# The second gate of an adaLN layer: from TensorE to VectorE's products in the down projection, with four engine orders laid out anew

## The chip, the cores and the metric

The kernel runs on one core of one Trainium2 chip. The metric is the device time of one execution in microseconds (us), the median of the runs shown.

## The reference

One layer of a diffusion backbone on 128 context tokens and 512 latent tokens of width 1024, all in fp32. A conditioning vector for each kind of token (c for the latent ones, c_ctx for the context) gives six modulation vectors of 1024; the last of them, g2, scales the output of the feed-forward part:

```python
mod = jax.nn.silu(cond) @ prm["w_ada"] + prm["b_ada"]
sh1, sc1, g1, sh2, sc2, g2 = [m[:, None, :] for m in jnp.split(mod, 6, axis=-1)]
h = rms_norm(x, prm["norm_mix_pre"]) * (1 + sc1) + sh1
...   # input projection, SSD mixer and Conformer branch -> mix = [y_ssd, u] @ w_out
x = x + g1 * rms_norm(mix, prm["norm_mix_post"])
h = rms_norm(x, prm["norm_ffn_pre"]) * (1 + sc2) + sh2
up = dwconv(h @ prm["w_ffn_up"])          # 2 x 2816 channels, 3x3 taps (latent), width 3 (context)
f_gate, f_val = jnp.split(up, 2, axis=-1)
f = (jax.nn.silu(f_gate) * f_val) @ prm["w_ffn_down"]
x = x + g2 * rms_norm(f, prm["norm_ffn_post"])
```

So g2 is needed only where the down projection's sums are scaled, at the very end. `w_ada` is 1024 x 6144.

## The kernel before

Channels lie on the 128 partitions, tokens on the free axis: T = 640 columns, 512 latent and 128 context. A fp32 product is three TensorE products of a high and a low part. Each weight unit (128x1024 or 128x768) is loaded by SP into a buffer `wr` (two of them), copied by ScalarE to `wh` (the high part, line 311) and subtracted by GpSimd (POOL) to `wl` (the low part, line 313); both have three buffers. Units are numbered in the order of use: 48 to 64 belong to the output projection, 65 to 108 to the up projection, 109 to 132 to the down projection.

The stages in the trace: input projection, SSD and convolutions until about 380 us; output projection until 492; the second normalisation (class `Mid`), with the first five up units woven in, until 542; up projection until 807, each unit followed by a convolution of nine taps (`up_conv`: the first tap by ScalarE, line 1227, the others by DVE, lines 1237 to 1240) which reads the unit's PSUM tile, of which there are three; down projection until 960; then the last normalisation, residual and the stores.

The modulation is computed in halves of 512 columns. `ada_load(i, tags)` loads eight tiles of 128x512 (256 KB each) of `wada2`; `ada_half(i, ws)` makes 64 small products on TensorE (line 460) with the activated conditioning (`cts`), copies the sum (line 463, `adar`), transposes it on TensorE (line 423) and adds the bias on DVE (line 432) into `modv[:, 48, 2]`. Halves 0 to 5 run in the output projection. Halves 6 and 7 are g2: half 6 is loaded into S0 to S7 and computed in the second normalisation, half 7 is loaded into H8 to H15 during the up projection and computed at its unit 11. `gg2` is g2 times the gain `g_ffn_post`, made by one DVE instruction. In `down_out(m)` ScalarE takes the Square of a finished tile (line 1412) and copies it scaled by `gg2[:, m, c]` (line 1418), for eight tiles m = 0 to 7 of 128 output channels.

The order of the instructions of each engine is not that of the program. `ORDER` holds a list for PE, DVE, Activation, Pool and SP, with the numbers of the program's instructions in the order in which the engine is to issue them, and `issue_in_order` chains them in this order. So an instruction that has to wait holds everything behind it on its engine.

Of the kernel before, what the change touches and what calls it, by code (L numbers as in the profile page):

```python
# [37 lines left out]
for _name, _w in (("b_ada", 48), ("g_mix_pre", 8), ("g_mix_post", 8), ("g_ffn_pre", 8),  # L38
# [48 lines left out]
3440-3442 3449-3451 3493-3504 3509-3510 3444-3445 3452 3511-3513 3539-3556 3455-3470 3477-3492 3514-3524  # L87
3505-3508 3557-3570 3525-3538 3453-3454 3572-3575 3644-3647 3668-3669 3576-3578 3648-3650 3670-3674
3579-3581 3571 3651-3653 3582-3584 3654-3656 3675-3680 3585-3587 3657-3659 3681-3682 3620-3623 3588-3590
3624-3625 3591-3593 3596-3598 3594-3595 3599-3619 3626-3643 3660-3667 3683-4059 4061-4081 4060 4082-5548  # L90
5597-5615 5549-5596 5616-5658 5693-5695 5659-5664 5696-5716 5665-5692 5717-6599 6665-6668 6600-6664
6669-6676""",
# [10 lines left out]
448-450 405-407 443 408-410 421-422 444 411 424 423 451 445-446 412-413 426 414-415 425 427 454 429-430 455  # L103
452-453 434 439 436 438 435 456 433 457 437 440 460 431 459 458 461-462 441 466-467 469-470 472 478 473
475-476 468 479-480 482-485 481 471 474 488 477 486 489 487 495 498 496 502 501 497 491 490 505 508 494
499-500 515 509 503-504 518 492 512 493 519 506-507 510-511 520-522 537 523 513-514 516 525 527-528 530 526
529 532-533 538 531 535 524 540 534 557 536 539 517 541-543 545 544 558 546 548 550 547 559 552 560-561
563-564 566 549 551 567 565 553 568 554-556 569 571-575 570 562 576-585 589 586-588 593 590 594 591-592 595
597 596 598 601-602 599-600 605 603-604 606-612 615-616 613-614 617-749 1053 750-1046 1049-1051 1047-1048
1052 1054-1063 1065 1064 1066-1075""",  # L110
# [15 lines left out]
477 442 440 416-417 478 427 419 413 428 420 418 421-424 479 425 480 443 426 482 481 483 465 449 451 450  # L126
452-453 455 454 484-485 457 469-470 487 459 486 456 466 460 468 458 461-462 467 463-464 488-489 492 490 495
498-499 494 502 496 491 497 493 505-506 509 500-501 503 507 510-511 504 512-514 516 515 508 525-526 528-529
527 521 517-518 532 519-520 531 523 522 524 530 542 541 533-536 544 543 550 537 545 538-540 547 546 559 551
548 553-554 560 556 555 549 552 557-558 561-565 568-569 566-567 570 578 571-577 581 579 583 580 603-605  # L130
609-611 582 584 588 585 615-616 632 617 586 621-622 633 590 589 634 587 643-644 638 592 623 591 645 639-640
596 593 649 624 650 598 594 597 601 599 651 595 652 606 600 602 613 607 612 608 618 614 625 619-620 627 626
630 628-629 635 631 641 636-637 646 642 653 647-648 655 654 658 656-657 660 659 663 661-662 665 664 668
666-667 670 669 673 671 675 672 674 678 676 680 677 679 683 681 685 682 684 688 686 690 687 689 693 691 695
692 694 698 696 700 697 699 703 701 727 705 702 704 708 706 709 707 714 710-713 715 719 716 725-726 717 720
731 718 723 721-722 732 724 728-729 733-734 730 735 741 736-740 745 742-744 746-747 751 748-750 752-753 757
754-756 758-759 763 760-762 764-765 769 766-768 770-771 775 772-774 776-784""",
# [1459 lines left out]
```

## Time and profile before

| what | us |
| --- | --- |
| median of 3 runs (lowest, highest) | 984.08 (983.13, 984.47) |
| span of the profiled execution | 979.4 |
| busy: PE, DVE, ACT, POOL | 944.5, 686.9, 471.3, 577.9 |
| share of PE in the chain that ended last | 87% |

The span is the time from the first to the last instruction of the profiled execution; what an execution takes outside it is in the runs' times alone, 4.7 us here by the difference to the median. Times of rows count from the span's start. PE is TensorE, DVE VectorE, ACT ScalarE, POOL GpSimd, SP the engine that issues the transfers. A name like `wh<-wr` says that a tile of the group `wh` is written from one of `wr`; numbers are left out.

### The profile page before, as it was taken

The numbers are of one execution on the slowest core, as the hardware profiler recorded it, in microseconds if no ns is written. First come the engines' busy times: TensorE is split into PE (matmuls) and PEld (weight loads), VectorE is DVE, ScalarE is ACT, GpSimd is POOL, SyncE is SP. The second block draws the span as 40 slices with busy tenths as digits, with TensorE's granted clock in tenths as the row PEclk, the third lists the DMA queues.
The fourth block names the chain that finished last, engine by engine and source line by source line (L and its number), as shares of the span: only waits on it lengthen the run. The fifth ranks groups of instructions, "written<-read, shape, count | busy, mean of one in ns | idle before, by whom it ended". The sixth has DMA issues, their size and how long they took to land.

```text
span 979.4 us, 18795 instructions
## 1 busy us (share of the span) xinstructions
PE 944.5 (96%) x7623; PEld 920.9 (94%) x7623; DVE 686.9 (70%) x1076; ACT 471.3 (48%) x799; POOL 577.9 (59%) x416
## 2 busy tenths in 40 slices
PE   4999999999999999999999999999999999999995
PEld 3799999999999998998889999999999999999995
DVE  1769898999989997523585998998988898400004
ACT  4355666877668477622464852323232336322211
POOL 1334699889999882534662994444454436543434
PEclk9999999999999999999999999999999999999998
DMA  9622424433424422578662322222222231322213
GB/s 347 250 72 86 117 82 127 146 95 123 139 80 142 128 91 93 196 244 303 200 218 88 129 86 69 84 78 73 86 66 86 66 87 54 94 69 76 82 38 108
DMA packets 50294, 117.52 MB, mean 120 GB/s; under 512 B 6016, under 2 KB 13952, under 8 KB 50208
## 3 DMA queue, kind: packets, MB, share of 16 engines
q1 hardware_dynamic: 50208, 116.33, 37.2%
q8 instruction: 60, 0.98, 0.4%
q14 instruction: 26, 0.21, 0.1%
HBM read 112.55 MB, written 3.75 MB: 119 GB/s over the span
## 4 chain that ended last, share of the span: by engine, by line
PE 87%; DMA 3%; ACT 3%; DVE 2%; SPq 1%; POOL 1%; issue 1%; POOLq 0%; ACTq 0%; DVEq 0%
PE ps L415 72%; PE ps L1259 3%; PE pq L415 2%; PE pq L818 2%; PE pq L807 1%; PE pq L460 1%; SPq L452 1%; DMA wr<-in_wout 1%; PE pq L744 1%; PE pq L441 1%; POOL wl L313 1%; PE pq L473 1%; DMA S<-acD 1%; ACT wh L311 1%; DMA T<-in_wada 1%
## 5 line engine op out<-in xcount | busy, mean ns | idle before, releaser
L313 POOL TENSOR_TENSOR wl<-wr,wh 128x1024 fp32r<-128x1024 f32 (+3 forms) x127 | 290.4, 2290 | 316.3 <-ACT wh L311 299.2
L415 PE MATMUL ps<-H,wh 128*128 128x384 f32 (+1 forms) x1636 | 315.7, 309 | 0.1
L311 ACT ACTIVATE wh<-wr 128x1024 fp32r<-128x1024 f32 (+3 forms) x131 | 131.3, 1003 | 316.2 <-PE ps L415 183.2
L415 PE MATMUL ps<-T,wh 128*128 128x384 f32 (+1 forms) x1472 | 272.5, 306 | 1.8 <-ACT S L1227 1.8
L1237 DVE SCALAR_TENSOR_TENSOR S<-ps,prms,S 128x441 f32<-128x441 f32 (+2 forms) x336 | 233.5, 695 | 29.4 <-ACT S L1227 18.9
L415 PEld LDWEIGHTS ps<-H,wh 128*128 128x128 f32 x1636 | 249.0, 188 | 2.7 <-issue 1.7
L415 PEld LDWEIGHTS ps<-T,wh 128*128 128x128 f32 x1472 | 218.9, 188 | 2.2 <-ACT S L1227 2.1
L872 DVE SCALAR_TENSOR_TENSOR ps<-u,prms,ps 128x655 f32<-128x655 f32 x205 | 185.1, 903 | 10.8 <-ACT ps L869 4.8
L415 PE MATMUL ps<-H,wl 128*128 128x384 f32 (+1 forms) x818 | 191.8, 309 | 0.0
L415 PE MATMUL ps<-T,wl 128*128 128x384 f32 (+1 forms) x736 | 166.2, 305 | 0.0
L415 PEld LDWEIGHTS ps<-H,wl 128*128 128x128 f32 x818 | 129.0, 188 | 1.0 <-issue 1.0
L415 PEld LDWEIGHTS ps<-T,wl 128*128 128x128 f32 x736 | 113.0, 188 | 0.0
L488 DVE RECIPROCAL rsm<-rsm 128x160 f32<-128x160 f32 (+2 forms) x9 | 7.4, 817 | 147.1 <-ACT rsm L487 147.1
L415 PE MATMUL ps<-S,wh 128*128 128x384 f32 (+1 forms) x420 | 88.0, 310 | 1.6 <-ACT wh L311 1.6
L415 PEld LDWEIGHTS ps<-S,wh 128*128 128x128 f32 x420 | 66.5, 188 | 2.8 <-ACT wh L311 1.8
L415 PE MATMUL ps<-S,wl 128*128 128x384 f32 (+1 forms) x210 | 54.9, 309 | 0.3 <-POOL wl L313 0.3
L789 ACT ACTIVATE S<-S,AC 128x128 f32<-128x128 f32 x140 | 45.5, 392 | 2.4 <-DMA S<-acD 2.4
L885 POOL TENSOR_TENSOR T<-T,T 128x640 f32<-128x640 f32 x20 | 32.0, 1602 | 12.5 <-ACT T L881 12.5
L1227 ACT ACTIVATE S<-ps,prms 128x640 f32<-128x640 f32 x42 | 36.5, 869 | 0.0
L415 PEld LDWEIGHTS ps<-S,wl 128*128 128x128 f32 x210 | 35.2, 188 | 0.9 <-POOL wl L313 0.5
L881 ACT ACTIVATE T<-u,prms 128x512 f32<-128x512 f32 (+1 forms) x54 | 27.9, 554 | 6.8 <-POOL T L885 6.8
L1339 POOL TENSOR_TENSOR H<-S,S 128x640 f32<-128x640 f32 x16 | 25.3, 1581 | 0.0
(346 smaller groups left out, 1180.3 us busy)
## 6 DMA issues: line engine op xcount, KB each, us to landing
wr<-in_wup SPq DMA_DIRECT2D x44, 512.0 KB, 3.5
wr<-in_win SPq DMA_DIRECT2D x36, 512.0 KB, 3.9
T<-in_wada SPq DMA_DIRECT2D x49, 256.0 KB, 5.4
S<-acD SPq DMA_DIRECT2D x28, 320.0 KB, 4.7
wr<-in_wdown SPq DMA_DIRECT2D x16, 512.0 KB, 3.4
wr<-in_wout SPq DMA_DIRECT2D x13, 512.0 KB, 4.5
H<-in_wada SPq DMA_DIRECT2D x23, 256.0 KB, 4.6
S<-in_wada SPq DMA_DIRECT2D x16, 256.0 KB, 5.4
```

Source lines behind the costliest of these rows:

```text
L311: ac.activation(hi[:, :n], raw[:, :n], AF.Copy)
L313: lo_eng.tensor_tensor(lo[:, :n], raw[:, :n], hi[:, :n].bitcast(F32), SUB)
L415: last_mm[0] = te.matmul(out, w, x[:, c0:c1], start=first and i == 0, stop=last and i == 2)
L789: ac.activation(rc, rc, AF.Relu, scale=-1.0, bias=AC2[:, c, row:row + 1])
L818: te.matmul(py[64 * h:64 * h + 64, i * P:(i + 1) * P], xt[:, c * P + 64 * h:c * P + 64 * h + 64], rs[h, d][:, c * P:(c + 1) * P], start=d ...
L872: ve.scalar_tensor_tensor(acc, u[:, j:j + UO], w(j), acc, MUL, ADD)
L881: ac.activation(t[:, b:c], u[:, a:a + c - b], AF.Copy, scale=w(j))
L885: gp.tensor_tensor(far, far, t, ADD)
L1227: ac.activation(out, v, AF.Identity, bias=prm_col("ffn_b", i), scale=w(1, 1))
L1237: ve.scalar_tensor_tensor(ob, vl[:, r0 + a - 1:r1 + a - 1, q0 + b - 1:q1 + b - 1], w(a, b), ob, MUL, ADD)
L1259: te.matmul(pt[:, o:o + c1 - c0], w[k] if i in (1, 2) else w[:, k * P:(k + 1) * P], x[:, c0:c1], start=k == 0 and j == 0, stop=k == KD - 1 ...
L1339: gp.tensor_tensor(f_raw[q], a, b, MUL)
```

## The change

Halves 6 and 7 of the modulation leave TensorE. In their place DVE computes g2 in the down projection: for each m, the 128 columns of `w_ada` that belong to its channels come transposed (channels on the partitions, 1024 conditioning inputs on the free axis, two loads of 128x512), and for each of the two conditioning vectors two instructions multiply them by the activated vector, broadcast to all partitions, and sum along the row (`accum_out`). So there are 32 such products, 8 sums of the two halves with the bias, and 8 scalings by the gain.

```diff
-    ada_w2 = ada_load(6, [f"S{k}" for k in range(8)])
...
-    ada_half(6, ada_w2)
...
+    def cond_rows():
+        for c in range(2):
+            for h in range(2):
+                t = slot(("S16", "S17", "U0", "U1")[2 * c + h])[:, 0:512]
+                src = idhl_d[P + 32 * c + 16 * h:P + 32 * c + 16 * h + 16, :].rearrange("a b -> (a b)")
+                sy.dma_start(t, src.unsqueeze(0).to_broadcast([P, 512]))
+                ac.activation(t, t, AF.Silu)
+                crows.append(t)
...
-        if i == 11:
-            g2_rest = ada_half(7, ada_w2, now=False)
-        if i == 14:
-            g2_rest()
-        if i == 5:
-            ada_w2 = ada_load(7, [f"H{8 + k}" for k in range(8)])
+        if i == 32:
+            cond_rows()
...
-    ve.tensor_tensor(gg2, modv[:, 40:48, :], prm_col("g_ffn_post", 0, 8).unsqueeze(2).to_broadcast([P, 8, 2]), MUL)
+    junk = sm.tile([P, T], F32, tag="tanh", name="junk", bufs=1)
+    gate_ws = []
+
+    def gate_load(m):
+        ws = []
+        for h in range(2):
+            t = slot((("S8", "S9") if m else ("H5", "H6"))[h])
+            sy.dma_start(t[:, 0:512], wada2[6 + m // 4, 2 * (m % 4) + h])
+            ws.append(t)
+        gate_ws.append(ws)
+
+    def gate_rows(m):
+        for c in range(2):
+            for h, w in enumerate(gate_ws[m]):
+                ve.scalar_tensor_tensor(junk[:, 0:512], w[:, 0:512], 1.0, crows[2 * c + h], MUL, MUL,
+                                        accum_out=modv[:, 2 * m + h, c:c + 1])
+        ve.scalar_tensor_tensor(modv[:, 40 + m, :], modv[:, 2 * m, :], prm_col("b_ada", 40 + m), modv[:, 2 * m + 1, :],
+                                ADD, ADD)
+        ve.tensor_scalar(gg2[:, m, :], modv[:, 40 + m, :], prm_col("g_ffn_post", m), None, MUL)
+        if 0 < m < KD - 1:
+            gate_load(m + 1)
+
...
+                i = DOWN_ORDER.index((m, g))
+                if i == 1:
+                    gate_load(0)
+                    gate_load(1)
+                for j in {3: (0,), 4: (1,), 5: (2, 3), 6: (4, 5), 7: (6, 7)}.get(i, ()):
+                    gate_rows(j)
```

On the host, c and c_ctx are appended to the input `idhl`, and the last two halves of `wada2` are transposed.

The lists in `ORDER` change from the output projection on. PE's list only loses the 66 instructions of halves 6 and 7. What the other lists do at the places that matter here, counted by instruction:

- ACT, output projection: the two copies `AT<-pq` (line 1030) that stood behind an activation of `T` into S13 (line 985) stand ahead of it. Second normalisation: the first tap of the first up convolution (S10, line 1227) stands ahead of the copy of weight unit 70, not behind it. Down projection: the scaled copies move behind later weight copies, that for m=1 ahead of `wh120`, that for m=2 ahead of `wh122`, and the Square of m=3 ahead of `wh122` too.
- DVE: the products of the gate stand behind one another, m=1 to m=7 without other work between; the scaling for m=1 comes within the products of m=5, the scaling for m=2 behind the last product of m=7. Those of m=0 lie between the taps of the last convolution. The tail's multiplications come first and its additions later.
- SP, output projection: the store of `nsb` (from S13) stands four places earlier; three of the `T` loads of `wada2` go earlier, six other loads go behind the load of weight unit 51. Down projection: the loads of the gate's halves stand between those of weight units 107 and 122; those of m=7 directly ahead of unit 122's.
- POOL: the additions to `m2sq` stand behind later weight units; the rest is nearly as before.

## Rows read from the trace of the kernel before

**Rows 1.** The page, parts 1 and 4: busy us; shares of the chain.

```profile
PE 944.5 (96%) x7623; PEld 920.9 (94%) x7623; DVE 686.9 (70%) x1076; ACT 471.3 (48%) x799; POOL 577.9 (59%) x416
...
PE 87%; DMA 3%; ACT 3%; DVE 2%; SPq 1%; POOL 1%; issue 1%; POOLq 0%; ACTq 0%; DVEq 0%
```

**Rows 2.** Windows by stage: length, busy us by engine, clock, DMA share.

```profile
420.00:492.00 72.00, 67.97 (x717) 64.11 (x715) 29.47 (x50) 26.32 (x44) 36.31 (x24) 1.00 0.73 244
...
591.00:640.00 49.00, 49.00 (x392) 48.60 (x392) 43.81 (x73) 15.86 (x19) 21.52 (x10) 1.00 0.23 76
...
850.00:905.00 55.00, 55.00 (x385) 55.00 (x384) 0.00 (x0) 13.18 (x18) 22.86 (x13) 1.00 0.28 80
```

**Rows 3.** Chain that ended last, 500 to 600: start, us, what.

```profile
517.31 1.08 PE pq L460 x33
...
522.39 1.00 PE pq L460 x28
...
529.22 0.11 PE pq L423
...
591.28 1.89 PE pq L460 x64
593.17 3.25 PE ps L415 x21
```

**Rows 4.** Timeline of PE; in brackets the idle time before.

```profile
399.97 1.30 PE L460 MATMUL pq<-H,cts 128*32 128x128 f32 x40 [0.98 <-ACT AT L1030]
...
454.70 0.97 PE L460 MATMUL pq<-T,cts 128*32 128x128 f32 x24 [0.74 <-DMA T<-in_wada]
...
457.34 0.52 PE L460 MATMUL pq<-T,cts 128*32 128x128 f32 x10 [1.03 <-DMA T<-in_wada]
...
533.66 0.28 PE L1259 MATMUL ps<-T,wh 128*128 128x256 f32 x1
...
542.49 0.82 PE L415 MATMUL ps<-T,wh 128*128 128x384 f32 x4 [1.76 <-ACT S L1227]
```

**Rows 5.** Timeline of ScalarE.

```profile
398.67 0.92 ACT L985 ACTIVATE S<-T,prms 128x640 fp32r<-128x640 f32 x1 [1.78 <-DMA out_nsb<-S]
...
534.03 1.06 ACT L311 ACTIVATE wh<-wr 128x1024 fp32r<-128x1024 f32 x1 [3.60 <-issue]
535.00 0.87 ACT L1227 ACTIVATE S<-ps,prms 128x640 f32<-128x640 f32 x1
```

**Rows 6.** Timeline of DVE.

```profile
531.06 0.60 DVE L1183 SCALAR_TENSOR_TENSOR T<-U,modv,T 128x128 fp32r<-128x128 f32 x2
...
535.90 5.81 DVE L1237 SCALAR_TENSOR_TENSOR S<-ps,prms,S 128x441 f32<-128x441 f32 x8 [4.23 <-ACT S L1227]
...
542.00 0.35 DVE L1240 SCALAR_TENSOR_TENSOR S<-ps,prms,S 128x127 f32<-128x127 f32 x1
...
586.67 0.35 DVE L1240 SCALAR_TENSOR_TENSOR S<-ps,prms,S 128x127 f32<-128x127 f32 x1
...
821.32 7.49 DVE L402 TENSOR_TENSOR H<-H,H 128x640 fp32r<-128x640 f32 x4
...
841.98 0.83 DVE L402 TENSOR_TENSOR H<-S,H 128x640 fp32r<-128x640 f32 x1
```

**Rows 7.** DMA issues: KB each, median us to landing; quiet stretch, then down projection.

```profile
S<-in_wada SPq DMA_DIRECT2D x2, 256.0 KB, 2.7
...
wr<-in_wdown SPq DMA_DIRECT2D x14, 512.0 KB, 3.4
```

**Rows 8.** Groups of DVE by shape: busy us, mean ns of one.

```profile
L574 DVE SCALAR_TENSOR_TENSOR S<-tanh,S 128x640 f32<-128x640 f32 x6 | 4.9, 824 | 1.3 <-ACT tanh L573 1.3
```

**Rows 9.** Timelines of ScalarE and POOL in the down projection.

```profile
890.50 0.69 ACT L1412 ACTIVATE AT<-ps 128x640 f32<-128x640 f32 x1
...
896.64 1.06 ACT L311 ACTIVATE wh<-wr 128x1024 fp32r<-128x1024 f32 x1 [4.62 <-issue]
...
885.71 2.41 POOL L313 TENSOR_TENSOR wl<-wr,wh 128x1024 fp32r<-128x1024 f32 x1 [4.48 <-ACT wh L311]
```

More of the change, by code (lines that the diff above doesn't have):

```diff
@@ L107 @@
[L107 to L110, printed above, removed]
+448-450 405-407 443 451 408-410 421-422 445 411 424 444 446 423 412 427 413 426 414-415 425 454 429 455 430
+452-453 438 433-434 456 437 435 457 436 439 458 460 459 440 461 431 462 441 466 478 467 469-470 472-473 475
@@ new lines @@
+468 476 479-480 483 482 484-485 474 481 471 477 487 486 490 488-489 495 498 496-497 491 501 494 505 502 492
+508 499-500 509 503-504 506 518 512 493 507 515 519 510-511 520-522 537 523 513 525 527 514 528 530 516 532
+529 526 517 533 531 538 535 524 536 534 540 557 539 541-543 545 544 558 546 548 550 547 559 549 551-553
+560-561 555 554 563-564 566-569 565 556 571-572 562 574 573 570 575-587 590 589 594 588 593 591-592 595-596
+599 597 601-602 598 600 603 606 604 607 610 605 608 614 613 609 612 611 615-633 635 634 636-653 655 654
@@ new lines @@
+656-659 665 660-661 666 662-664 667-673 675-676 674 677-683 685-687 684 688-693 695 694 696-702 705 703-704
+706-752 755 753 756 754 757-772 775 773-774 776-793 795-796 794 797-810 815 811-813 816 814 817-822 825 823
+826 824 827-833 835 834 836-842 845 843 846 844 847-851 855 852-854 856-863 865-866 864 867-881 885 882-884
+886-890 895 891-892 896 893 897-898 894 899-900 905 901 906 902-904 907-913 915-916 914 917-930 935 931-932
+936-937 933 938 934 939-943 945-949 944 950-952 955-959 953-954 960-973 975 974 976-981 1045 982-990 1049
@@ new lines @@
+991 995 992-994 996-1001 1005 1002-1003 1006-1010 1004 1011-1014 1019-1022 1015 1017 1016 1023 1018 1024
+1029 1025-1026 1031 1030 1032-1033 1027 1034 1028 1035 1047 1046 1036-1039 1050 1040-1042 1051-1052 1043
+1053 1044 1048 1054-1059 1061-1064 1067-1070 1073 1071 1074-1075 1072 1076 1065 1077 1079 1078 1080-1081
+1060 1082-1083 1085-1086 1084 1087-1088 1091-1094 1066 1089 1095-1096 1090 1097-1098 1100 1102 1099 1104
+1106 1101 1108 1103 1105 1109 1111 1113 1115 1107 1117 1110 1112 1116 1114 1118""",
@@ L130 @@
[L130 to L134, printed above, removed]
@@ new lines @@
+625 628 618 626 633 629 627 639 634 644 635 640 651 645-646 652-654 656 658 657 659 661 655 660 662-664 666
+668 665 667 671 669-670 673 672 674 676 678 677 679 681 675 687 682 680 688 690 689 691-693 695-697 700 698
+694 701 699 729 703 702 706 705 708 707 710 704 709 711 716 712 727 714 713 721 717-718 715 723 720 719 722
+733 725 728 724 731 734 726 730 735-736 732 738 737 740 743 747 744 748 750 749 739 745 753-754 746 756 751
+755 752 741 759 757-758 760 762-763 761 742 764-768 771 769 772 770 773-774 777-778 780-781 779 775 782
@@ L138 @@
+785-786 783 776 784""",
     "Pool": """
@@ L1548, in _layout @@
     out["cst"] = cst
-    out["idhl"] = np.concatenate([np.eye(32, dtype=f32)] * 4, axis=0)
+    out["idhl"] = np.concatenate([np.eye(32, dtype=f32)] * 4 + [a["c"][0].reshape(32, 32), a["c_ctx"].reshape(32, 32)])
     w = a["w_ada"][0].reshape(4, 2, P, 6, 4, 2, P)
@@ L1554, in _layout @@
     w = a["w_ada"][0].reshape(KD, P, 6, 2, 512)[:, :, 2:6]
-    out["wada2"] = w.transpose(2, 3, 0, 1, 4).reshape(8, KD, P, 512)
+    w2 = w.transpose(2, 3, 0, 1, 4).reshape(8, KD, P, 512)
+    g2 = a["w_ada"][0][:, 5 * D:].T.reshape(KD, P, 2, 512).transpose(0, 2, 1, 3).reshape(2, KD, P, 512)
+    out["wada2"] = np.concatenate([w2[0:6], g2])
     w = a["w_in"][0]
```

57 lines of the change are left out of this document (27 added, 30 removed).

## The prediction

> **What bounds the kernel now.** I read the page first: its busy times and its chain. TensorE is busy for 944.5 us of a span of 979.4, and 87% of the chain that ended last is PE [rows 1]. So a microsecond taken from PE's own stream counts wherever PE never waits. The windows by stage say where that is: from 591 to 640 and from 850 to 905 PE is busy for the whole window (the stretches between are alike), and in the second of these DVE does nothing at all, while DMA moves at a share of 0.28 [rows 2]. In the output projection PE loses 4 of 72 us and DMA stands at 0.73. Third come PE's own waits in order of time. They lie where an activation, a load or the first convolution is late [rows 4]; the last before the down projection's end is at 542.49. Last I followed the two new orders, instruction by instruction, against these times.
>
> **PE work removed, half 7.** Its 64 small products take 1.89 us in the chain at 591.28 [rows 3]; the transposition that goes with them I price like that of half 6, 0.11. PE is full afterwards [rows 2], and DVE keeps pace: PE takes the tile of its next unit at 593.17 [rows 3], and the convolution that frees it (three units back) had ended at 587.0 [rows 6], 6 us before. So nothing else fills the gap: **-2.0 us**.
>
> **Half 6 and the wait at 542.49.** The products lie in two pieces, 1.08 and 1.00, and the transposition takes 0.11 [rows 3]: 2.2. Behind them PE waits 1.76 for its sixth up unit [rows 4], which needs the PSUM tile that the first convolution reads; DVE leaves that tile at 542.00 + 0.35 [rows 6]. The convolution starts at 535.90, behind ScalarE's first tap (535.00, 0.87), which stands behind the copy of a weight unit (534.03, 1.06) [rows 5]. The new ACT order has the tap ahead of the copy, so the convolution starts 0.94 earlier by itself and 2.2 earlier because PE reaches the tile's end earlier: 3.1 at most. DVE's normalisation of the second half runs beside the last piece; its last tile is ready at 531.06 + 0.60 [rows 6] and PE takes it at 533.66 [rows 4], 2.0 later. 1.1 of this goes with the last piece and the transposition, and the new order has DVE make some of the eight tiles up to three instructions later (0.8 us): at most 0.9 is lost. I take **-3.0** (bounds -2.2 and -3.1).
>
> **Output projection.** Here only the orders change. Waits that they touch: 0.98 at 399.97, where PE waits for a copy that ScalarE makes late because it sat 1.78 on a store [rows 4, 5]; the new ACT order has the copies ahead of that activation, and SP issues the store four places earlier. At 454.70 and 457.34 PE waits 0.74 and 1.03 for conditioning weights [rows 4]; the new SP order lets three of these loads go earlier, but it puts six others behind a unit's load, in a stage where DMA is busy three quarters of the time [rows 2]. Sum of what can go: 0.98 + 0.74 + 1.03 = 2.75; everything named and 0.7 of small gaps around it give 5. If the moved loads are late instead, one more wait of the size of 1.03. I take **-2.0** (bounds +1 and -5).
>
> **Second gate on DVE: what is added.** 32 products of 128x512 with a row sum, 8 small sums, 8 scalings; 16 loads of 256 KB, the same in number and size as the removed ones; four broadcast loads and four Silu, issued near 600 us where ACT has 33 us idle in 49 [rows 2] and the needed slots are free: 0. The nearest row to the product is L574, also two SBUF sources into SBUF: 0.824 us for 640 columns [rows 8]; the same operation with 127 columns takes 0.35 [rows 6], so a column costs 0.92 ns and 512 columns 0.71. The row sum is shown by no row; from below it costs nothing, from above it doubles the streamed part (0.47 more). I take 0.71, since the same operation without it is the nearest.
>
> All this lies beside PE if the chain is in time. It is one chain: from m=1 all loads go into the same two slots, so each pair waits for the four products of the pair before. One round: issue 0.4, landing 3.4 (a 512 KB unit's time in this stage [rows 7], the upper bound; 2.7 for two quiet loads of this size is the lower), then three products that don't overlap the landing, 2.1, sums and semaphores 0.35: 6.3. DVE is free at 842.8 [rows 6]. First round with all four products: 842.8 + 3.9 + 2.9 = 849.6; six more give 887.4, and the scaling for m=2, which the new DVE order puts behind the last product of m=7, comes near **889**.
>
> Who waits: in ACT's new order the scaled copy for m=2 stands ahead of the split of weight unit 122, and so does the Square of m=3, which PE's end of that tile allows at 890.50 [rows 9]. Queued behind them: the copy of unit 122 (1.06), then its low part on POOL (2.41), then PE, which starts that unit at 896.64, when the buffer of unit 121 comes free [rows 9]. Backward: 896.6 - 2.4 - 1.1 - 0.65 (the scaled copy) = 892.4 at the latest, so 3.4 us of slack. On SP the load of unit 122 stands behind the loads of m=7 (about 882), lands by 886, and is in time. The other scaled copies have more room (m=1 about 5 us).
>
> What can eat the 3.4: DVE and POOL. At 821.32 four DVE subtractions with both sources in SBUF, beside a busy POOL, take 7.49 us, against 0.83 for one of them at 841.98 [rows 6]; so 4.2 us are lost in 7.5. In the chain DVE works for 45% of a round and POOL for 22 of 46 us (nine units of 2.41 or less [rows 9]); lost share 0.56 x 22 x 0.45 = 5.5 us. Against it the lower landing gives 7 x 0.7 = 4.9. An estimate of both: 0 to 2 us of stall. I take **+0.8** (bounds 0 and +3, without the half rate below).
>
> The Trainium skill, "SBUF — State Buffer", section "Who interferes with whom", calls the port that DVE and GpSimd share an exclusive lock; the trace agrees in kind (7.49 us for four). By it alone the products would lose all of POOL's time that falls into their part of a round, 22 x 0.45 = 9.9, and the stall would be 9.9 - 4.9 - 3.4 = 1.6 instead of 0.8, the time 978.7; by the row's share it is 0 to 2.
>
> **Tail.** Reordered, same work: the adds later, the multiplications first. 0 (bounds -0.5 and +0.5).
>
> **Sum.** -2.0 - 3.0 - 2.0 + 0.8 + 0 = -6.2. The profiled execution's span is 979.4; the median of the runs shown, 984.08, lies 4.7 above it, and I let these 4.7 stand. 984.1 - 6.2 = **977.9 us**. From no change one can tell about 0.2%, 2.0 us.
>
> **Rivals.** (1) *The chain at half rate: slower.* If the product with a row sum runs at half speed, 0.47 more each, some 25 of the 28 products count in full (three a round and the first): 889 + 11.8 = 900.8. DVE then works for 60% of a round and loses 0.56 x 22 x 0.6 = 7.4 to POOL, against 4.9 from the loads: 903.3, 10.9 past 892.4. PE stalls there once by 10.9; with the rest at -7.0 the time is 984.1 + 3.9 = 988. It decides from about 1.0 us a product on, where the stall reaches the 7.0. For it: the row of L574 has no row sum. Against it: the same two sources at full rate, 0.824 for 640 [rows 8].
>
> The Trainium skill has this as a rule: "Vector Engine (DVE) Microarchitecture Reference", section "7. Points that are easy to get wrong", says that this instruction with two sources in SBUF that are not bf16 halves its throughput, as no port is left for the accumulator. L574's 0.824 us speaks against it for instructions without a row sum; none here shows one with it.
>
> (2) *The orders of the output projection give nothing, or cost.* The gain there is 0 and the chain costs 2: -2.0 - 2.6 + 0 + 2 = -2.6, 981.5, still faster. For it: DMA at 0.73, with loads moved behind others. (3) *All given back:* loads moved behind others cost 1 more, and the chain's stall is 3: -4.6 + 1 + 3 = -0.6, 983.5, the same. (4) *More than forecast:* the whole 5 of the projection, no stall: -10, 974. (5) *The removed products cost nothing on PE* (another wait takes their place): against it stands that PE is full from 591 on, so half 7 must show; I leave it inside (3).
>
> **How the numbers follow.** The forecast, 975 to 980, 0.60; (2), 980 to 982, 0.12; (3) 0.09; (4), below 975, 0.07; (1) 0.12. Faster by over 0.2%: 0.60 + 0.12 + 0.07 = 0.79; same 0.09; slower 0.12. The range leaves out the half rate (0.12) and the far end of (4) (0.03): 974 to 985, and the time itself is that of the forecast.
>
> **What would show it.** Right: no L460 rows after 500; PE's wait before its sixth up unit gone or below 1, and the unit some 3 us earlier beside the end of the output projection; the up projection shorter by 2.0 at 591; the new DVE products at 0.7 to 0.85 between 805 and 885, PE without a gap or with one below 2 near unit 122; the first stage boundary after the output projection 1 to 4 us earlier. Wrong: products above 1.1 us; a PE wait for ScalarE's split near 885 to 900 by over 4; loads of conditioning weights later at 450 to 460 than before; a convolution start that does not move.

## The result: slower by 0.5%

The changed kernel takes 986.60 us (median of 7 runs, 984.54 to 991.53), the kernel before 982.62 on the same chip (7 runs, 979.07 to 984.47). The ratio is 1.0046, 95% interval 1.0026 to 1.0066: slower, where 977.9 and faster were predicted, and outside the range of 974 to 985. The profiled execution of the changed kernel spans 983.7 us and took 985.5, so 1.8 lie outside a span and not 4.7 (1.8 to 2.0 in every run here). The profile of before (979.4) must then be an execution of about 981.2, quicker than before's median.

First the page of the changed kernel, parts 1 and 4, against [rows 1].

```profile
PE 943.2 (96%) x7493; PEld 919.2 (93%) x7493; DVE 709.6 (72%) x1151; ACT 472.8 (48%) x801; POOL 576.0 (59%) x416
...
PE 79%; DMA 8%; DVE 5%; ACT 4%; issue 1%; POOL 1%; SPq 1%; DVEq 0%; ACTq 0%; POOLq 0%
```

PE has 130 instructions less and yet only 1.3 us less of busy time: some of those that are left ran longer. And its share of the chain fell from 87% to 79%. So work left PE, and waits and slower stretches came. Where, shows PE's timeline (start, duration, and in brackets the wait ahead of it):

```profile
403.65 0.42 PE L470 MATMUL pq<-H,cts 128*32 128x128 f32 x8 [0.85 <-DMA H<-in_wada]
...
433.93 0.44 PE L425 MATMUL ps<-S,wl 128*128 128x384 f32 x1 [0.44 <-POOL wl L323]
...
446.80 0.86 PE L470 MATMUL pq<-T,cts 128*32 128x128 f32 x24 [0.47 <-DMA T<-in_wada]
...
485.62 0.50 PE L425 MATMUL ps<-S,wh 128*128 128x256 f32 x2 [1.92 <-ACT wh L321]
...
488.58 0.39 PE L425 MATMUL ps<-S,wl 128*128 128x256 f32 x1 [0.68 <-POOL wl L323]
...
492.69 0.39 PE L425 MATMUL ps<-S,wh 128*128 128x256 f32 x1 [2.07 <-DVE M L1168]
...
545.78 0.82 PE L425 MATMUL ps<-T,wh 128*128 128x384 f32 x4 [0.88 <-DVE S L1250]
...
843.32 0.56 PE L425 MATMUL pq<-S,wh 128*128 128x384 f32 x2 [0.56 <-DVE S L412]
```

Against [rows 4]: the wait of 1.76 before the sixth up unit is 0.88 now, as forecast. The waits of 0.98, 0.74 and 1.03 in the output projection are not gone: others stand in their place (0.85, 0.44 and 0.47 are shown; with 0.27 at 441.51 and 0.22 at 458.58 they sum to 2.25 of the 2.75). The waits at 485.62 and 488.58 (1.92 and 0.68) were there before, somewhat shorter:

```profile
483.45 0.50 PE L415 MATMUL ps<-S,wh 128*128 128x256 f32 x2 [1.59 <-ACT wh L311]
...
486.01 0.39 PE L415 MATMUL ps<-S,wl 128*128 128x256 f32 x1 [0.28 <-POOL wl L313]
```

New are 492.69 and 843.32.

A second reading is used throughout below, the *offset*: both programs have the same PE instructions apart from the removed ones, so each one's start can be compared with its start in the profile of before. The sixth up unit, for example, starts at 542.49 before and 545.78 after: +3.29. Each row is one execution, each column a time of before; "end" is the span's end.

| kernel | 380 | 480 | 498 | 542 | 600 | 841 | 905 | end |
| --- | --- | --- | --- | --- | --- | --- | --- | --- |
| after | +3.0 | +1.8 | +6.4 | +3.3 | +0.8 | +0.8 | +2.6 | +4.3 |
| e5, no products | +2.1 | +2.2 | +5.1 | +2.0 | -0.3 | -0.2 | -0.2 | +1.6 |
| e9, gate chain laid out anew | +5.8 | +5.6 | +8.7 | +5.6 | +3.3 | +3.3 | +4.2 | +5.9 |
| e11, before's orders, new program | -0.4 | -0.4 | +0.0 | -1.9 | -4.2 | -4.2 | -4.2 | -3.3 |
| e12, halves 6 and 7 left out of before | -0.4 | -1.6 | -1.0 | -2.9 | -3.6 | -3.6 | -3.6 | -2.8 |
| e13, e11 with new projection orders | +1.1 | +2.7 | +5.7 | +3.7 | +2.8 | +2.8 | +2.8 | +3.3 |

What stands at 345 (+2.7 in after, -0.4 to +2.6 in the others) is chance: no instruction ahead of it was changed. The new orders begin a little ahead of the output projection, on DVE at 351 and on ScalarE and SP by 372; from 345 to 380 most executions with them lose 0.3 to 0.5 (e8 1.6, e9 3.2), those with before's orders there at most 0.1. Only the differences between columns are read. After loses 4.6 between 480 and 498, gains 3.1 until 542 and 2.5 until 600, loses 1.8 between 841 and 905 and 1.7 in the tail.

### The profile page after: what moved, and what is told of

The parts are those of the page before. It is cut to its first block, busy times and chain, and to the rows that moved or that the text cites. A ratio compares the mean times of both kernels' runs of the same rounds, so it can differ in the third digit from the quotient of the medians.

```text
span 983.7 us, 18619 instructions
## 1 busy us (share of the span) xinstructions
PE 943.2 (96%) x7493; PEld 919.2 (93%) x7493; DVE 709.6 (72%) x1151; ACT 472.8 (48%) x801; POOL 576.0 (59%) x416
## 4 chain that ended last, share of the span: by engine, by line
PE 79%; DMA 8%; DVE 5%; ACT 4%; issue 1%; POOL 1%; SPq 1%; DVEq 0%; ACTq 0%; POOLq 0%
PE ps L425 67%; PE ps L1269 3%; DMA H<-in_wada 2%; DMA T<-in_wada 2%; PE pq L828 2%; PE pq L817 1%; DMA wr<-in_wout 1%; PE pq L754 1%; DMA S<-acD 1%; PE pq L425 1%; ACT wh L321 1%; DVE S L1247 1%; POOL wl L323 1%; DMA S<-in_wada 1%; DMA T<-in_xT 1%
## 5 line engine op out<-in xcount | busy, mean ns | idle before, releaser
L1419 DVE SCALAR_TENSOR_TENSOR junk<-S,S 128x512 f32<-128x512 f32 x14 | 13.5, 962 | 25.2 <-DMA S<-in_wada 25.1
```

The source lines that it names most:

```text
L1419: ve.scalar_tensor_tensor(junk[:, 0:512], w[:, 0:512], 1.0, crows[2 * c + h], MUL, MUL, accum_out=modv[:, 2 * m + h, c:c + 1])
```

## The experiments

All times are medians in us, with the lowest, the highest and the number of runs; ratios are to the kernel before on the same chip.

| run | time | ratio, 95% interval |
| --- | --- | --- |
| after | 986.60 (984.54-991.53, 7) | 1.0046 [1.0026, 1.0066] |
| e1_copy_first | 992.24 (986.22-996.88, 6) | 1.0085 [1.0057, 1.0113] |
| e2_tail_before | 988.51 (983.82-993.10, 9) | 1.0055 [1.0033, 1.0077] |
| e3_gate0_later | 987.59 (981.65-991.50, 11) | 1.0043 [1.0023, 1.0063] |
| e4_all_three | 985.64 (979.75-992.75, 12) | 1.0027 [1.0006, 1.0049] |
| e5_no_products | 982.90 (980.35-984.94, 12) | 0.9996 [0.9982, 1.0010] |
| e6_orders_alone | 989.24 (988.09-995.25, 6) | 1.0075 [1.0055, 1.0095] |
| e7_load_ahead | 985.60 (982.05-991.18, 12) | 1.0028 [1.0011, 1.0045] |
| e8_four_edits | 981.48 (978.97-985.05, 12) | 0.9986 [0.9974, 0.9999] |
| e9_deadline | 983.75 (981.44-987.09, 12) | 1.0006 [0.9990, 1.0022] |
| e10_five_edits | 980.84 (978.17-982.23, 12) | 0.9975 [0.9959, 0.9990] |
| e11_old_front | 978.31 (975.82-983.11, 12) | 0.9955 [0.9938, 0.9972] |
| e12_halves_out | 978.51 (975.93-983.17, 12) | 0.9958 [0.9941, 0.9975] |
| e13_new_oproj | 984.22 (981.65-986.32, 12) | 1.0012 [0.9998, 1.0026] |
| e14_new_up | 978.21 (975.80-980.54, 9) | 0.9954 [0.9938, 0.9970] |
| e15_new_tail | 980.25 (977.50-983.35, 12) | 0.9975 [0.9961, 0.9989] |
| e16_new_to480 | 980.97 (977.60-984.71, 12) | 0.9981 [0.9960, 1.0002] |
| e17_new_480 | 981.91 (980.10-984.94, 12) | 0.9997 [0.9978, 1.0016] |
| e18_copy_ahead | 981.38 (979.46-985.61, 12) | 0.9989 [0.9970, 1.0008] |

My theory after the first result: the removed work is worth what was predicted, and the new orders give it back at three places (ScalarE's copy of weight unit 63 at 490, the first gate products between the last convolution's taps at 843, the tail), with a stall of the gate chain besides. The rival: the 32 products on DVE cost it, wherever they stand.

### Three places, one at a time (e1 to e4)

e1 moves ScalarE's copy of weight unit 63 (529) ahead of three squares of the residual (521, 518, 520), where before had it; e2 gives the tail before's order on all four queues; e3 puts the products for m=0 behind the last convolution's work; e4 is the three together.

```diff
 e1, "Activation":
-... 528 521 518 520 529 519
+... 528-529 521 518 520 519
 e2, "DVE", and likewise the ends of "Activation", "Pool" and "SP":
-... 1098 1100 1102 1099 1104 1106 1101 1108 1103 1105 1109 1111 1113 1115 1107 1117 1110 1112 1116 1114 1118
+... 1098-1106 1108 1107 1109-1118
 e3, "DVE":
-... 990 1049 991 ... 1039 1050 1040-1042 1051-1052 1043 1053 1044 1048 1054
+... 990-991 ... 1039-1044 1048-1054
```

> The changed kernel with one instruction moved: ScalarE's copy of weight unit 63 stands again ahead of the three squares of the second normalisation, where the kernel before has it. Theory A (the copy is what PE waits for at 492.69; the squares hold it while DVE's additions are slowed beside POOL, and after the wait PE's clock falls): PE's wait of 2.07 us there shrinks below 0.5, the granted clock between 489 and 498 stays at 1.00, the first product of the up projection comes 3 to 4 us earlier, and the time is 3 to 4 us below the changed kernel's, near 983. Rival B (DVE's slowed additions and the PSUM evictions behind them are the limit, the copy only ends at the same moment): PE waits at the same place for DVE, and the time is within 1 us of the changed kernel's.

> The changed kernel with the orders of the tail (DVE, ScalarE, POOL and SP from the last normalisation on) as in the kernel before. Theory A (the multiplications first and the additions last crowd DVE and POOL at the end and make the stores late): from PE's last spread to the end of the span 9 us as before instead of 11.4, and the time 2 us below the changed kernel's, near 984.5. Rival B (the tail is longer because the down projection hands it over differently): the tail stays at 11 us and the time does not change.

> The changed kernel with DVE's products of the first gate tile (m=0) moved behind the last low parts of the gated values. Theory A (these four products, two of them slowed beside POOL, make the low part late that PE waits for at 843.32, and PE runs some 5% slower for the 14 us after that wait): the wait of 0.56 goes, PE's distance to the kernel before does not grow by 1 us between 842 and 860, and the time is 1 to 1.6 us lower, near 985.2. Rival B (DVE's subtractions are late by themselves, slowed beside POOL): the wait stays. Rival C (PE's slower pace has another cause, DMA or DVE traffic): the wait goes and the pace after it stays slow, 0.5 us gained.

> All three edits together on the changed kernel. If the places are independent, their gains add: 986.6 - 3.5 - 2 - 1.4, near 979.7, below the kernel before by 2 to 4 us. If the loss of the changed kernel lies in the first 170 us (its profile is 3 us behind the kernel before's there, with nothing changed in that stretch), the three together bring less and the time stays near 983, no better than the kernel before.

In the profiled executions each edit did its part: in e1 PE starts its sixth up unit at 542.36 instead of 545.78; in e2 the tail is again as long as before; in e3 the wait at 843 is gone. The medians of e1 to e3 show none of it, and e1 is even the slowest kernel of all; e4's ratio is 0.0019 below after's where 0.007 was expected, within the intervals. What can take the gain, e3's trace shows; it is of an execution of 990.9, near its longest. ScalarE's timeline first, then PE's, then the windows with PE's busy time, granted clock, DMA share and GB/s:

```profile
886.01 0.69 ACT L1460 ACTIVATE H<-ps,gg 128x512 f32<-128x512 f32 x1 [12.07 <-DVE gg L1423]
886.60 1.78 ACT L321 ACTIVATE wh<-wr 128x768 fp32r<-128x768 f32 x2
```
```profile
887.49 0.86 PE L425 MATMUL ps<-S,wh 128*128 128x384 f32 x4 [1.91 <-ACT wh L321]
889.38 0.90 PE L425 MATMUL ps<-S,wl 128*128 128x384 f32 x2 [1.04 <-POOL wl L323]
```
```profile
870.00:888.00 18.00, 16.09 (x112) 1.00 0.36 113
888.00:892.00 4.00, 2.96 (x12) 0.57 0.32 117
892.00:896.00 4.00, 4.00 (x18) 0.58 0.15 29
896.00:905.00 9.00, 8.72 (x60) 1.00 0.43 151
```

ScalarE sits 12.07 us on the scaled copy for m=1, whose gain DVE has not written; two weight copies stand behind it; PE waits 1.91 and 1.04 and then runs 8 us at a granted clock of 0.57 to 0.58, so mostly at the lower of its two levels (1.2 and 2.4 GHz). e3's offset grows by 7.2 from 870 to 905, against 0.35 in the profile of after, 4.4 in e1 and 2.9 in e4. So the gate chain misses its deadline by an amount that differs from execution to execution. That fits the spread of e1 to e4, 9 to 13 us, where before on the same chip spreads over 5.5 in 25 runs (980.48 to 985.93), though this is only argued. What a typical execution of e1 spends is not shown: its profiled one (986.2) was its quickest.

### What the products and the orders cost (e5, e6, e12)

e5 is the changed kernel without the second gate's 16 loads, 32 products and 8 sums (its values are left out). e6 is before's program, halves 6 and 7 included, with the new orders. e12 is before with halves 6 and 7 left out and its orders else kept (here too the values of the gate are left out).

```diff
 e5, in gate_load and gate_rows:
-            sy.dma_start(t[:, 0:512], wada2[6 + m // 4, 2 * (m % 4) + h])
-                ve.scalar_tensor_tensor(junk[:, 0:512], w[:, 0:512], 1.0, crows[2 * c + h], MUL, MUL, ...)
-        ve.scalar_tensor_tensor(modv[:, 40 + m, :], ...)
 e6, all lists:
-ORDER of before
+ORDER of after, the instructions of halves 6 and 7 behind their neighbours in before's lists
 e12, in before:
-    ada_w2 = ada_load(6, [f"S{k}" for k in range(8)])
-    ada_half(6, ada_w2)
-            g2_rest = ada_half(7, ada_w2, now=False)
-            g2_rest()
-            ada_w2 = ada_load(7, [f"H{8 + k}" for k in range(8)])
```

> The changed kernel without the 16 loads, the 32 products and the 8 sums of the second gate; the 8 scalings stay and take another modulation vector, so the output leaves out g2. All orders stay otherwise. Theory A (the chain of loads and products ends at the very moment at which the split of unit 122 needs it, so that PE stalls in some executions and not in others, by up to 3 us and a lower clock after it): PE has no wait between 845 and 960, the runs lie within some 5 us of each other as the kernel before's do (980.5 to 985.9), instead of 984.5 to 991.5, and the median falls to 983 to 984.5. Rival B (the orders alone are what costs): the median stays at 986 to 987 and the spread with it.

> The kernel before with the new orders of DVE, ScalarE, POOL and SP, and the second gate still on TensorE (halves 6 and 7, their loads, copies and additions stay behind the instruction that precedes them in the old order). By theory A the orders cost 3.7 at the copy of unit 63 and 2.2 in the tail and give 0.9 in the output projection and 0.9 at the first convolution: 4 us above the kernel before, near 987, with the kernel before's small spread (5 us), since no chain of products is there. If the gate's chain is what makes the changed kernel slow (rival), the orders alone are no slower than the kernel before: 983 or less.

> The kernel before with halves 6 and 7 of the second modulation simply left out on TensorE, VectorE, ScalarE and the queue (16 loads, 32 matmuls, the copies and sums; the second gate takes the rows of an earlier part, so its values are left out), orders else as before. It prices what the change takes away, with nothing put in its place. Theory: 5 us less than before, 977.5 to 978.5, of which 2.2 lie at 590 to 600. Rival (half of the wait at half 6 is filled by the weight units behind it): 3 us less, 979.5 to 980.5.

These three with after make a chain of ratios. Taking halves 6 and 7 out: 0.9958, 4.1 us less of 982.6. The new orders on top, without products (e5): 0.9996, 3.7 given back. The products on top of that (after): 1.0046, 4.9 more. The sum is +4.5, the result. e6 agrees with the middle term's sign and is larger, 0.0075 or 7.4 us; its trace has a PE wait of 2.83 at 521.82 for a POOL result that no other kernel here shows, so part of it may come from where I put half 6's instructions in the new lists.

### The gate chain (e7 to e10)

Why is the chain late? DVE's timeline of after at m=2, and SP's:

```profile
851.76 1.36 DVE L1419 SCALAR_TENSOR_TENSOR junk<-S,S 128x512 f32<-128x512 f32 x1 [1.66 <-DMA S<-in_wada]
...
859.91 0.69 DVE L1419 SCALAR_TENSOR_TENSOR junk<-S,S 128x512 f32<-128x512 f32 x1 [6.79 <-DMA S<-in_wada]
```
```profile
845.09 4.38 SPq L1412 DMA_DIRECT2D S<-in_wada  x2
852.60 3.13 SPq L297 DMA_DIRECT2D wr<-in_wdown  x2
855.82 0.38 SPq L1412 DMA_DIRECT2D S<-in_wada  x1
```

and of SP's waits from 838 to 862 (total, times, longest):

```profile
SPq L297 <- POOL wl L323: 9.6, 4, 3.1
```

The second load of m=2 stands on SP behind the loads of weight units 117 and 118, which wait until POOL is done with their buffers; it goes out at 855.82, and DVE stands idle for 6.79. In ScalarE's timeline of after the end of it reads so:

```profile
895.30 0.69 ACT L1460 ACTIVATE S<-ps,gg 128x512 f32<-128x512 f32 x1 [2.32 <-DVE gg L1423]
```

The gain for m=2 comes just ahead of 895.3, where 889 was predicted; its deadline was estimated at 892.4, before's time, which is 894.6 here by the offset of 2.2 at 870. The load of unit 122 is as late: SP issues it behind the loads of m=7, at 889.76, and it lands 6.0 us later, at 895.8, where the prediction had it in by 886. e7 moves the load ahead of the two weight units. e8 is e4 and e7 together. e9 leaves fronts and tail as in after and lays out the chain alone: sums and scalings directly behind each m's own products, the scaled copies of m=2 behind `wh` of unit 123, the load of unit 122 ahead of m=7's. e10 is e8 with the edits of e9.

```diff
 e7, "SP":
-... 319 326 331 320 334
+... 319-320 326 331 334
 e9, "DVE", "Activation", "SP":
-... 1059 1061-1064 1067-1070 1073 ... 1076 1065 1077 ... 1081 1060 1082 ... 1066 1089 ... 1097
+... 1059-1097
-... 756 751 755 752 741 759 757
+... 756 755 741 759 751-752 757
-... 329 333 332 337
+... 329 337 333 332
```

> The changed kernel with one transfer moved on SP: the second load of m=2 stands directly behind its first, ahead of weight units 117 and 118, behind which the products of m=2 waited 6.8 to 8.2 us for it. Theory A (this wait uses up the slack of the chain): the second product of m=2 starts 6 to 8 us earlier, the scaling for m=2 ends near 889 and not at 895 to 901, PE does not wait between 885 and 905, the runs' spread shrinks and the median falls by 2 to 3, to 984. Rival B (the chain is not what the runs differ by): the chain is earlier and time and spread stay.

> The load moved as in the kernel with one transfer moved, and the three edits of the first group (the copy of unit 63 ahead of the squares, the tail's old orders, the first gate tile's products later). If the chain was what held the three edits back at 985.6 with a spread of 13 us: 980 to 981.5, below the kernel before's 982.8, with a spread of about 5. If not: near 985 with the same spread.

> The changed kernel with the gate chain alone laid out anew: VectorE sums and scales each row block of the second gate right behind that block's own products, ScalarE does the two scaled copies of block 2 behind the copy of weight unit 123 instead of ahead of it, and SyncE issues the load of unit 122 ahead of the second-to-last gate load. Theory (the chain's lateness is an affair of its order and of the queue, and costs 0.3 to 7 us from one execution to the next): no TensorE wait between 870 and 905, the time near that of the kernel without products plus the wait at 843, 983 to 984.5, and a spread between runs near before's 5 instead of 7. Rival (VectorE beside GpSimd is too full for 32 products wherever they stand): another wait of 1 us or more takes the place, 985.5 to 987.

> The four edits (copy of unit 63 first, tail as before, first row block's products later, second load of block 2 ahead) and the deadline edits of the run beside it. Theory: the remaining wait of 1.55 at the end of the down projection goes, 979.5 to 980.5, faster than before by 0.25 to 0.35%. Rival (the wait is filled by the clock or by another wait): 981 to 982, as the four edits alone.

e7's theory did not hold. The second product of m=2 starts at 852.08 instead of 859.91, as expected, but the next load then takes the wait. DVE's first product of m=3 in e7 shows it:

```profile
862.52 1.00 DVE L1419 SCALAR_TENSOR_TENSOR junk<-S,S 128x512 f32<-128x512 f32 x1 [6.17 <-DMA S<-in_wada]
```

The gain for m=2 is ready at 895.4 in e7 and at 895.3 in after, not near 889, and the ratio (1.0028) is below after's by less than the intervals allow to tell. e7's profile still has a PE wait of 1.45 at 899.56, e8's one of 1.55 at 896.50, both for unit 122's low part. In e9 PE is full where it stalled, though its last products run until 902.8; ScalarE's copies that need the late gains wait without anything of PE's behind them. e9's windows and ScalarE:

```profile
841.00:870.00 29.00, 28.43 (x198) 1.00 0.40 119
870.00:905.00 35.00, 35.00 (x246) 1.00 0.46 144
```
```profile
894.83 1.05 ACT L321 ACTIVATE wh<-wr 128x1024 fp32r<-128x1024 f32 x1
...
902.13 1.78 ACT L1460 ACTIVATE S<-ps,gg 128x512 f32<-128x512 f32 x4 [2.53 <-DVE junk L1419]
```

So the orders, that is what stands behind the late chain, and not the products, were the cost: e9 takes the ratio from 1.0046 to 1.0006, 3.9 us of the 4.9. Its three edits were not tried apart, so the shares of the scaled copies and of unit 122's load stay open. The 28.43 of 29.00 holds the wait at 843, which e9 kept. e10 is faster than before, 0.9975.

### The orders in front and behind (e11, e13 to e18)

e11 has the changed program, before's orders everywhere except for the gate (with the edits of e3, e7 and e9). e13 to e17 put the new orders of one stretch each back into it: e13 the output projection from its first new order up to 502, e16 and e17 the two parts of that, up to 480 and from 480 to 502; e14 508 to 545; e15 the tail. e18 is e13 with unit 63's copy ahead of the squares.

```diff
 after to e11, all lists:
-ORDER of after
+ORDER of before, the gate's instructions placed as in e9, with e3 and e7
 e11 to e17, "Activation" at 480 (DVE and Pool likewise):
-... 508 525-526 528-529 527 521 517-518 532 519-520
+... 508 526 525 528 521 518 520 529 519 524 527 532 517
 e11 to e14, "Pool" (DVE, ScalarE and SP likewise):
-... 274 279 275 280 276-277
+... 274-275 280 276 279 277
 e11 to e15, "DVE" (the other three likewise):
-... 1098-1106 1108 1107 1109-1118
+... 1098 1100 1102 1099 1104 1106 1101 1108 1103 1105 1109 1111 1113 1115 1107 1117 1110 1112 1116 1114 1118
 e13 to e18, "Activation":
-... 528 521 518 520 529 519
+... 528-529 521 518 520 519
```

> The changed program with before's orders on every queue up to the gate loads and in the tail, the products of the gate in the changed kernel's places with the later first block, the second load of block 2 ahead, and the deadline edits. Theory (what halves 6 and 7 give is kept when nothing else is laid out anew; the new orders of the output projection give nothing): PE ahead of before by 3 at 542 and by 5 at 600, end 977 to 978.5. Rival (the new orders from the output projection on carry a part of the gain, as the prediction held): 979.5 to 981, no better than the five edits.

> The program of the old front (978.31), with the changed kernel's orders put back from the start of the output projection to the copy and squares behind it (up to 502), nothing else. Theory (weight unit 63's copy stands behind squares that wait for sums slowed beside GpSimd; the orders ahead of it give nothing): 3 us more, 980.5 to 982.5, the TensorE waits and the lower granted clock of 485 to 498 back. Rival (the new orders give a part of the predicted 2 us in the projection and lose it at 490): within 1 us of the old front.

> The program of the old front, with the changed kernel's orders put back between 508 and 545 alone, the start of the up projection. Theory (the wait for ScalarE's modulated slice halved there, 0.88 instead of 1.76): 0.9 to 1.2 us less, 977 to 977.5. Rival (what is gained there is lost in the norm ahead of it): the same time as the old front, 978.3.

> The program of the old front, with the changed kernel's orders put back from 931 on alone: the last row block's sums, scalings and stores. Theory (VectorE's three last sums stand behind the scalings and run beside GpSimd): 2 us more, 980 to 980.8, with the span's end 11 us behind the last TensorE reduction instead of 9. Rival (the tail's length in one execution is chance): the same time as the old front, 978.3.

> The program of the old front (978.3), with the changed kernel's orders put back up to 480 alone: the output projection's transposes, second-modulation loads, products and sums, without the copy and squares behind. Theory (these orders give and cost nothing): 978 to 979.5. Rival (they hold up the projection by the 1.6 that the trace of the run before showed between 380 and 480, or more): 980 to 982.

> The program of the old front, with the changed kernel's orders put back from 480 to 502 alone, where ScalarE copies weight unit 63 behind three squares and not ahead of them. Theory (the copy stands behind squares that wait for VectorE's sums beside GpSimd): 2.5 to 3.5 more, 981 to 982, a TensorE wait of 2 or more at 490. Rival (VectorE's sums are late only where the orders ahead of 480 are new too): within 1 of the old front.

> The whole output projection in the changed kernel's orders (984.2), with one instruction moved: ScalarE copies weight unit 63 ahead of the squares, as before did. Theory (the copy's place is most of the cost): 2.5 to 3.5 less, 980.5 to 981.5. Rival (the lateness comes from the sums and not from the copy): 983.5 to 984.5.

e11 takes 978.31, as fast as e12 (978.51), which makes no second gate at all. PE's windows of e11 have no idle time from 541 to 905, though all 32 products are made in them:

```profile
541.00:841.00 300.00, 300.00 (x2088) 1.00 0.27 83
841.00:870.00 29.00, 29.00 (x204) 1.00 0.40 124
870.00:905.00 35.00, 35.00 (x245) 1.00 0.39 124
```

Against e11 (0.9955), the new orders cost 5.6 us in the output projection (e13), 2.0 in the tail (e15) and nothing at the up projection's start (e14). Between 550 and 841 they were not put back alone; there the offset falls by 1.9 to 2.2 in every kernel without half 7, whatever its orders. Each ratio is uncertain by about 0.0016, so each such difference by some 2 us; e13's stands clear of zero, e15's only with its trace, below.

Within the projection, e17 alone costs 4.1 and e16 2.6 (not clear of zero), about e13's 5.6 together. At 480 ScalarE, DVE, POOL and PE of e17 read:

```profile
491.35 1.35 ACT L1169 ACTIVATE T<-M 128x384 f32<-128x384 f32 x3 [5.77 <-DVE M L1168]
492.60 0.51 ACT L321 ACTIVATE wh<-wr 128x384 fp32r<-128x384 f32 x1
```
```profile
484.52 4.91 DVE L1168 TENSOR_TENSOR M<-M,T 128x384 f32<-128x384 f32 x2
...
491.24 0.41 DVE L1082 TENSOR_TENSOR M<-ps,T 128x256 f32<-128x256 f32 x1
```
```profile
484.00 5.00 POOL L323 TENSOR_TENSOR wl<-wr,wh 128x1024 fp32r<-128x1024 f32 x2
```
```profile
493.16 0.39 PE L425 MATMUL ps<-S,wh 128*128 128x256 f32 x1 [2.05 <-DVE M L1168]
```

and the same instructions of e11:

```profile
485.36 0.52 ACT L321 ACTIVATE wh<-wr 128x384 fp32r<-128x384 f32 x1 [2.09 <-DMA wr<-in_wrest]
```
```profile
481.19 2.59 DVE L1168 TENSOR_TENSOR M<-M,T 128x384 f32<-128x384 f32 x2
...
484.75 0.41 DVE L1082 TENSOR_TENSOR M<-ps,T 128x256 f32<-128x256 f32 x1
```

In the new order the copy of unit 63 (`wh`, 128x384) stands behind squares that need DVE's additions, and two of these take 4.91, each beside one of POOL's two low parts; in e11 only the first lies beside one (2.12) and the second takes 0.55, 2.59 in all; the copy comes 7 us later, and PE, which needs it, waits 2.05. DVE's release of a PSUM tile (L1082) comes 6.5 later too. With the copy ahead (e18) PE still waits there, now for this release:

```profile
489.82 0.36 PE L425 MATMUL ps<-S,wh 128*128 128x256 f32 x1 [1.98 <-DVE M L1082]
```

so e18 gets back 2.3 us by the medians' ratios and not 5.6, and 0.6 in its profile between 480 and 498. All executions with the copy in the new place lose 2.5 to 4.6 there, those with it ahead (e1, e4, e8, e10, e18) 1.3 to 2.4, those with before's orders at most 0.6. e16's 2.6 are not located: its profiled execution shows no loss between 380 and 542 that e11 does not have, and its interval overlaps e11's. Over all profiled executions, the fourteen with new orders from 345 to 480 range there from 0.9 gained to 3.1 lost (mean 0.9 lost), the five with before's from 1.2 gained to 1.4 lost (mean 0.2 gained). The tail, DVE's timeline of e15 and then of e11, the three last additions of S tiles:

```profile
971.20 2.66 DVE L1489 TENSOR_TENSOR S<-S,M 128x256 f32<-128x256 f32 x3
973.79 0.41 DVE L1489 TENSOR_TENSOR U<-U,M 128x256 f32<-128x256 f32 x1
```
```profile
969.58 0.50 DVE L1489 TENSOR_TENSOR S<-S,M 128x256 f32<-128x256 f32 x1
...
971.31 0.50 DVE L1489 TENSOR_TENSOR S<-S,M 128x256 f32<-128x256 f32 x1
972.18 0.50 DVE L1489 TENSOR_TENSOR U<-U,M 128x256 f32<-128x256 f32 x1
```

0.89 apiece where the additions are gathered at the end beside POOL's, 0.50 where they alternate with multiplications that read PSUM. POOL is busy beside both, so why the gathered ones take longer is argued and not shown. From PE's last products (966.55 and 966.02) to the end of the span are 11.8 in e15 and 10.1 in e11. This stretch takes 11.2 to 11.8 in all eight executions with the new tail and 9.2 to 10.3 in all twelve with the old one.

The parts do not add up exactly. e13's and e15's costs on e11 give 7.6, while e5 against e12 gives 3.7. One reason is in the offsets: with the old up orders PE waits 1.76 before its sixth up unit, and in some executions its granted clock is lower after that (e12, e13, e17, e18; in e13 0.89 and 0.86 in 543 to 548 and 548 to 556), which costs 1.3 to 1.5 between 542 and 550; in others it is not (e11, e15, e16). The new up orders wait 0.88 and lose nothing there (after, e1 to e10), except e14, which waits another 0.87 at 548.42 and loses 1.1. What is left is within the intervals.

## Why the prediction was wrong

**Half 7 and half 6: right.** The offset falls by 2.2 at 593 in every kernel without half 7 (predicted 2.0), and by 3.1 between 498 and 542 in after (predicted 3.0). Of these 3.1 the removal gives 2.0 with before's orders (e11), and the new order the other 1.1 (predicted 0.9); in the times this 1.1 is not seen (e14 against e11). e12 as a whole, which only removes, gives 4.1 by its ratio and 4.6 by the medians.

**Output projection, -2.0 (bounds +1 and -5): the step that failed.** I counted the three named waits as gone and looked for the danger in the loads. The waits were replaced by others of nearly the same sum, so the gain up to 480 is nothing or a small loss, and the main loss stands behind it, at 480 to 498, in a part of the new ACT and DVE orders that I had not followed to the copy of unit 63: +2.5 to +4.6 in the profiled executions, 4.1 by e17, 5.6 with the stretch ahead (e13). Of after's 4.6, 2.8 are longer and new PE waits and some 1.5 (an estimate from the products' distances below) the lower clock behind the last of them.

**Tail, 0 (bounds -0.5 and +0.5): wrong**, +2.0 (e15; 1.7 by its trace). I priced the same work at the same durations; gathered beside POOL the last additions take 0.89 and not 0.50.

**Second gate, +0.8 (bounds 0 and +3): right in mechanism, mis-sized.** It costs 4.9 as it stands (after against e5). In the round of 6.3 each load is issued when its slot is free; that SP's weight loads, which wait for buffers, hold loads of the chain is missing from the working. It is 6.8 idle us at m=2 in after, and 6.2 at m=3 where that load is moved (e7); with the offsets taken off, the gain for m=2 comes at 893.0 in after and 894.7 in e7, behind the forecast 889 by more than the slack of 3.4. The load of unit 122, which the working had in by 886, is held by the same chain and lands at 895.8. And m=0's products were placed at nothing: between the last convolution's taps they make PE wait 0.56 at 843. By the offsets that place costs 0.8 to 0.9 in e1, e2, e7 and e9 and 1.5 in after.

**Price of a product, 0.71: right; rival (1) fell.** The changed kernel's rows, DVE's groups by shape (count, busy, mean ns):

```profile
L1419 DVE SCALAR_TENSOR_TENSOR junk<-S,S 128x512 f32<-128x512 f32 x14 | 13.5, 962 | 25.2 <-DMA S<-in_wada 25.1
L1419 DVE SCALAR_TENSOR_TENSOR junk<-S,U 128x512 f32<-128x512 f32 x14 | 9.7, 690 | 0.4
L1419 DVE DVE_READ_ACCUMULATOR junk<-S,U 128x1 f32 x14 | 1.1, 82 | 0.0
```

Undisturbed, as in the second row, a product takes 690 ns, and a separate read of the row sum 82. The first row has the same work at 962 on average: some of its products lie beside POOL's work and take up to 2.37 us; the prediction counted that as a loss of its own. The Trainium skill, "Vector Engine (DVE) Microarchitecture Reference", section "7. Points that are easy to get wrong", has this instruction at half throughput with two sources in SBUF that are not bf16; the trace differs, and the measurement decides.

**Base, 984.1 with 4.7 outside the span:** 1.5 too high, as before's median over 7 runs is 982.62. Of the rivals, (1) has the nearest time (988) by a mechanism that did not occur; (3), "all given back" (983.5), has the stall, at too small a size, and a loss in the projection, which it puts down to the loads. (2) lets the projection's orders cost, but prices them at 0; that the orders alone could make the kernel slower had no rival.

## What to carry to other kernels

Price a reordering by what it puts behind a waiting instruction, queue by queue, up to the next instruction that the bounding engine needs; here one weight copy behind three squares, weight copies and a weight load behind a late chain, and additions gathered beside POOL's turned a planned gain of 6 us into a loss of 4. Change one thing at a time: with the orders left as they were, moving the gate gives all that taking out halves 6 and 7 can give (e11, 978.31, ratio 0.9955), faster than both kernels, and none of the new stretches of order improves on it. Work that is hidden is free only if nothing urgent stands behind its consumers: in e9 the same late chain costs PE nothing from 870 on, with the weight copies and a weight load ahead of what waits for it.

## What the runs showed of the hardware

A PE wait can cost more than its length. After the wait at 492.69 the windows of the changed kernel (PE busy, granted clock) show it:

```profile
485.00:492.00 7.00, 4.32 (x32) 1.00 0.38 105
492.00:495.00 3.00, 2.31 (x16) 0.85 0.05 5
495.00:498.00 3.00, 3.00 (x18) 0.58 0.48 169
```

PE had been busy for 4.32 of 7 us; from 494.1 to 497.5 its products come 0.21 apart and not 0.12, and the granted clock is 0.58 in a window where PE is busy throughout. e17 has the same 4.32 us and a wait of 2.05, and its clock stays at 1.00:

```profile
495.00:498.00 3.00, 3.00 (x46) 1.00 0.56 175
```

So not every such wait does it, and what decides it is not shown. After the shorter wait at 843 the pairs of products of the changed kernel come 0.300 apart instead of 0.287 for some 12 us, with a granted clock of 1.00 in the rows: a slower pace that the clock column does not show. The wait alone does not explain it: e1, e2, e7 and e9 have the same wait of 0.56 and keep before's pace.

A tiny DVE instruction can take as long as the POOL instruction beside it. In e18, DVE and then POOL:

```profile
481.00 2.21 DVE L1136 TENSOR_SCALAR gs<-modv 128x16 f32<-128x16 f32 x1
```
```profile
480.82 2.35 POOL L323 TENSOR_TENSOR wl<-wr,wh 128x1024 fp32r<-128x1024 f32 x1
```

It ends 0.04 behind POOL's. In e11, where POOL's instruction beside it had 0.10 to go, it takes 0.17. The Trainium skill, "SBUF — State Buffer", section "Who interferes with whom", says of the port pair that DVE shares with GpSimd: whoever issues first gets it for the whole instruction, and the other fully blocks. The two cases agree. So the share of 0.56 that the prediction took from one row of before says little of a single instruction: where the order puts it decides.
